# Seven half-size products for 9 of 11 pairs of feature blocks in a half-step FFN

## The chip, the core and the metric

The kernel runs on one core of a Trainium2 chip. The metric is the device time of one execution in microseconds. The engines named here are PE (TensorE, the matmuls), PEld (its weight loads), DVE (VectorE), ACT (ScalarE), POOL (GpSimd) and SP (SyncE, which issues most transfers). SBUF is the on-chip memory, PSUM the memory into which PE sums.

## The reference

The kernel computes two layers of an encoder for 512 tokens of width 1024. Each layer has three sublayers: a half-step FFN, a mixer, a second half-step FFN. The change is in the FFNs, whose core is

```
h = modulate(x, shift, scale)                       # x * (1 + scale) + shift, (512, 1024)
gate, up = jnp.split(h @ w_in, 2, axis=-1)          # w_in (1024, 2 * 2816)
y = (jax.nn.silu(gate) * up) @ w_out                # w_out (2816, 1024)
x = layer_norm(ALPHA * x + 0.5 * g * y, ln_g, ln_b)
```

Shift, scale and g of every sublayer come from a vector c: `mod = silu(c) @ ada_w[l] + ada_b[l]`, with ada_w[l] of 1024 x 9216. The mixer projects h by another matrix, runs a state-space scan, an attention and a short convolution on parts of it, and projects back. Everything is float32.

## The kernel before

**Precision.** A float32 product is made of three matmuls in float32r. Each operand is split into a high part (ACT copies it, rounded) and a low part (DVE subtracts the high part), and `mm3` adds low x high, high x low and high x high in PSUM. The helper `split` makes the parts of 1024 weights per partition, in tiles hi and li (input weights) or ho and lo (output weights).

**A half-step FFN** (`ffn`) goes over 11 pairs of blocks of 256 features: a pair is 256 gate columns and 256 up columns of w_in. For each, `cols_unit` loads two units of 1 MB (rows 0 to 1023, 256 columns), splits them in halves, and 2 x 2 blocks of 128 features by 512 tokens are summed in four PSUM banks over 8 row blocks: 96 matmuls of 512 columns. The first pair of a half-step runs on 256 tokens at a time, so that it can begin before the last token tile is ready. ACT makes silu of the gate (sg), DVE multiplies by up (af), and the result is split into ah and al. The pairs go in two groups (0 to 5, 6 to 10). After each group `out_proj` multiplies its features by the rows of w_out, for four token tiles and two halves of 512 columns, and `fold` adds gate times the result to x, two DVE instructions for each tile and half. After the second group come LayerNorm's statistics and normalization (`ln_norm`) and, by `modulate`, the transposed and modulated input hh, hl of the next sublayer.

**The affine of LayerNorm** (`x_affine`: x times g plus b) runs on POOL, 16 instructions of 128 x 512 to a sublayer, at pair 1 of an FFN and in the middle of a mixer.

**adaLN in the background.** `ada_acc` loads 1024 columns of ada_w in eight row blocks of 512 KB (ra) and sums them, weighted by silu(c), in two DVE instructions a block (acc). `ada_gate` and `ada_ss` (scale and shift) then split the sums and add them over the partitions on PE. These are Python generators; `begin` queues them at the start of an FFN, and `tick`, called at each of 33 weight units, advances them by a credit of 2.7 or 1.3 steps. A first FFN of a layer has three modules for itself and those after it, six sums of eight blocks in half-step 0; the last FFN has one sum.

**Buffers.** `rawp` holds two raw weight units of 8 KB per partition, `adap` two ada blocks, `whp` and `wlp` six high and six low halves each, `lp` 28 tiles of 2 KB for activations and vectors, `tp` nine temporaries. PSUM is two pools of four banks.

**Order.** Instructions are written in program order; a scheduler orders each engine by this priority among what its own timing finds ready, and adds the semaphores. Each engine then runs its list in order. Only the start of the first sublayer (`start`) is ordered by hand.

Of the kernel before, what the change touches and what calls it, by code (L numbers as in the profile page):

```python
# [8 lines left out]
F32 = mybir.dt.float32  # L9
# [18 lines left out]
NLONG = 28  # L28
NTMP = 9
NW = 6  # L30
# [3 lines left out]
CR = (2.7, 1.3)  # L34
WSZ = 1072
# [6 lines left out]
class InOrder:  # L42
    """An engine whose instructions are issued in program order while it is on."""
# [25 lines left out]
def trunk(ctx, tc, x, c, ln_in_g, ln_in_b, ada_w, ada_b, ffn1_w_in, ffn1_w_out,  # L69
# [8 lines left out]
    rawp = ctx.enter_context(tc.tile_pool(name="rawp", bufs=2))  # L78
    adap = ctx.enter_context(tc.tile_pool(name="adap", bufs=2))
# [6 lines left out]
    psa = ctx.enter_context(tc.tile_pool(name="psa", bufs=4, space=bass.MemoryType.PSUM))  # L86
    psb = ctx.enter_context(tc.tile_pool(name="psb", bufs=4, space=bass.MemoryType.PSUM))

    def pa(shape, name):
        return psa.tile(shape, F32, tag="a", name=name)  # L90

    def pb(shape, name):
        return psb.tile(shape, F32, tag="b", name=name)
# [128 lines left out]
    def ada_acc(l, col):  # L222
        """acc[p, f] = sum_k silu(c)[8p + k] * ada_w[l, 8p + k, col + f], row by row."""
        w = ada_w[l].rearrange("(p k) f -> p k f", k=KD)
        acc = [slot([P, 512], F32, f"acc{l}_{col}_{h}") for h in range(2)]
        for k in range(KD):
            raw = adap.tile([P, D], F32, tag="ra", name=f"ra{l}_{col}_{k}")
            sp.dma_start(raw, w[:, k, col:col + D])
            for h in range(2):
                rk = raw[:, h * 512:(h + 1) * 512]  # L230
                if k == 0:
                    after(dve.tensor_scalar(acc[h], rk, cT[:, 0:1], None, op0=ALU.mult), ln_done[0])
                else:
                    dve.scalar_tensor_tensor(acc[h], rk, cT[:, k:k + 1], acc[h],
                                             op0=ALU.mult, op1=ALU.add)
# [4 lines left out]
    def acc_split(acc):  # L240
        """The high and low part of each half."""
        parts = []
        los = adap.tile([P, 2, 512], F32R, tag="ra", name="gl")
        for h in range(2):
            hi, lo = tmp([P, 512], "gh", F32R), los[:, h]
            act.activation(hi, acc[h], AF.Copy)
            dve.tensor_tensor(lo, acc[h], hi.bitcast(F32), ALU.subtract)
# [3 lines left out]
    def acc_sum(ps, hi, lo):  # L251
        """The sum over the partitions, on every partition."""
# [7 lines left out]
    def mod_finish(s, a, b, psc, pss):  # L260
        """Features a*128 to b*128: scale and shift folded with the LayerNorm in front."""
# [39 lines left out]
    def ada_first(part, which):  # L301
        """The row blocks of the first sublayer's scale (1) or shift (0) for one range of features."""
        w = ada_w[0].rearrange("(p k) f -> p k f", k=KD)
        kk, nk = FIRST[part]
        n, nb = nk * P, (2, 1, 4)[part]
        c0 = which * D + kk * P
        raws = []
        for k in range(0, KD, nb):
            if part > 0:
                raw = slot([P, nb, n], F32, f"rf{part}_{which}_{k}")  # L310
            else:
# [5 lines left out]
    def sum_first(part, raws):  # L317
        """The sums over the row blocks, one vector instruction at a time."""
# [49 lines left out]
    credit = [0.0, 0.0]  # L368

    def begin(*gens):  # L370
        """Queue background work, to be spread over the 33 weight units of a half-step FFN."""
        pending.extend(gens)
        credit[0] = 0.0
        credit[1] = len(pending) and CR[0] if len(gens) > 2 else CR[1]

    def tick():
        credit[0] += credit[1]
        while pending and credit[0] >= 1:
            try:
# [4 lines left out]
                pending.pop(0)  # L384

# [8 lines left out]
    def load(w, c0, r0, k, n, name):  # L394
        """Rows r0 to r0 + 128 k, columns c0 to c0 + n, as [128, k, n]."""
        raw = rawp.tile([P, 2048], F32, tag="raw", name="r" + name)
        v = raw[:, :k * n].rearrange("p (k f) -> p k f", f=n)
        sp.dma_start(v, w[r0:r0 + k * P, c0:c0 + n].rearrange("(k p) f -> p k f", p=P))
        return v

    last = [None]

    def split(v, name, prev=None):
        """One half unit, any view [128, a, b] of raw weights, as high and low parts."""
        a, b = v.shape[1], v.shape[2]
        wh = whp.tile([P, WSZ], F32R, tag="wh", name="h" + name)[:, :a * b].rearrange("p (a b) -> p a b", b=b)
        wl = wlp.tile([P, WSZ], F32R, tag="wl", name="l" + name)[:, :a * b].rearrange("p (a b) -> p a b", b=b)
# [4 lines left out]
    def cols_unit(w, c0, name, prev=None):  # L412
        """256 columns of a [1024, .] matrix, two halves [128, 8, 128]."""
        v = load(w, c0, 0, KD, 256, name)
        return [split(v[:, :, j * P:(j + 1) * P], f"{name}_{j}", prev) for j in range(2)]

    def rows_unit(w, r0, c0, nk, name, prev=None):
        """128 nk rows by 512 columns, halves [128, 2, 512]."""
        v = load(w, c0, r0, nk, 512, name)
        return [split(v[:, 2 * j:2 * j + 2, :], f"{name}_{j}", prev) for j in range(nk // 2)]  # L420
# [8 lines left out]
    def ln_stat(t, h, st, piece=None):  # L429
        """Statistics of 512 columns, or of one half of them."""  # L430
# [17 lines left out]
    def finish(t, st):  # L448
        """The last LayerNorm, stored."""
# [9 lines left out]
    def ln_norm(t, st):  # L459
        """xt[t] <- (xt[t] - mean) * rstd."""  # L460
# [5 lines left out]
    def modulate(s, t, qq=(0, 1), prev=None):  # L466
        """hT[:, :, t] = the transposed modulation of xt[t] for sublayer s."""
        ts = slice(t * P, (t + 1) * P)
        for q in qq:
# [7 lines left out]
            hf = tmp([P, 4, P], f"hf{s}_{t}_{q}")  # L477
# [13 lines left out]
    def modulate_first(kk, ps):  # L491
        """hT[:, kk, :] for the first sublayer; yields before the vector part."""
        hf = tmp([P, T], f"hf0_{kk}")
# [3 lines left out]
        ln_done[0] = dve.tensor_tensor(hT[1][:, kk, :], hf, hT[0][:, kk, :].bitcast(F32), ALU.subtract)  # L497

# [4 lines left out]
    def ln_in(t):  # L503
        """The first LayerNorm of one token tile; yields between its vector parts."""
# [10 lines left out]
    def start():  # L515
        """Up to the first pair of the first sublayer, by ranges of features."""
# [10 lines left out]
        v = [load(ffn1_w_in[0], 0, 0, KD, 256, "i0_0_0")]  # L527
        raws.append(ada_first(1, 1))
        v.append(load(ffn1_w_in[0], DFF, 0, KD, 256, "i0_0_1"))
        raws[1] += ada_first(1, 0)  # L530
        raws.append(ada_first(2, 1) + ada_first(2, 0))
        v.append(load(ffn1_w_in[0], 256, 0, KD, 256, "i0_1_0"))
# [9 lines left out]
        def lo(which, j):  # L542
            units[which].append(split(v[which][:, :, j * P:(j + 1) * P], f"{("i0_0_0", "i0_0_1", "i0_1_0")[which]}_{j}"))
# [9 lines left out]
        def products(k, whiches=(0, 1)):  # L553
            for which in whiches:
                for j in range(2):
                    wh, wl = units[which][j]
                    mm3(banks[which][j], wh[:, k, :], wl[:, k, :],
                        hT[0][:, k, :], hT[1][:, k, :], k == 0, k == KD - 1)
# [26 lines left out]
        lo(0, 1)  # L585
# [10 lines left out]
        lo(1, 0)  # L596
# [22 lines left out]
        lo(2, 1)  # L619
# [4 lines left out]
        return banks, units[2]  # L624

    def x_affine(s, eng):
# [558 lines left out]
```

## Time and profile before

| | |
|---|---|
| device time, median of 2 runs | 2028.8 us (2028.63 to 2028.97) |
| span of the profiled execution | 2026.3 us |
| around the span, against the median | 2.5 us |
| matmuls | 9462 |
| DVE, ACT, POOL busy | 1190, 689, 218 us |
| moved by the transfers | 264 MB |

The profile names instructions by the tile that they write and read (`pf<-hh,hi` is a matmul into pf with the moving operand hh and the weights hi). Nearly all instructions are issued through one helper on line 52, so groups are told apart by tiles, not lines. A mean duration contains the time that an instruction spends in the pipeline beside its neighbours; the price of one instruction in a row of equal ones is the distance of their starts.

### The profile page before, as it was taken

What the parts mean: (1) busy time and instruction counts of PE and PEld (TensorE: products, weight loads), DVE (VectorE), ACT (ScalarE), POOL (GpSimd) and SP (SyncE); (2) the same over time, 40 slices, a digit from 0 to 9 for tenths busy, and PEclk for the clock granted to TensorE, in tenths of its full rate; (3) what the DMA queues carried; (4) which work ended last, traced back from release to release, by engine and by line L of the source; (5) the groups of instructions that cost most, each with busy time, mean ns of one, the idle gap of its engine ahead of it and who ended that gap; (6) DMA issues with size and microseconds to landing.
All of it is one profiled execution on the core that took longest, in us unless ns stands there. A gap on an engine that the chain in (4) does not pass through costs nothing.

```text
span 2026.3 us, 23498 instructions
## 1 busy us (share of the span) xinstructions
PE 1980.4 (98%) x9462; PEld 1624.8 (80%) x9462; DVE 1190.0 (59%) x1728; ACT 688.5 (34%) x1092; POOL 218.2 (11%) x182
## 2 busy tenths in 40 slices
PE   5999999999999999999999999999999999999998
PEld 4777878898877888888898788888977798888887
DVE  8896663467666655543477757436666575433336
ACT  3332132164454422122152322323544453222220
POOL 0230000007000040000004000000350004000000
PEclk9999999999999999999999999999999999999999
DMA  9765552333211544432345746322322144223331
GB/s 322 232 208 208 177 166 73 95 92 117 83 63 53 182 155 158 149 106 92 104 162 173 240 157 235 104 84 81 122 80 73 53 137 136 102 84 103 104 104 42
DMA packets 178540, 263.98 MB, mean 130 GB/s; under 512 B 9612, under 2 KB 124672, under 8 KB 178432
## 3 DMA queue, kind: packets, MB, share of 16 engines
q1 hardware_dynamic: 173936, 254.97, 37.7%
q10 hardware_dynamic: 4496, 7.52, 1.2%
q8 instruction: 74, 1.21, 0.2%
q14 instruction: 34, 0.28, 0.0%
HBM read 260.37 MB, written 2.10 MB: 130 GB/s over the span
## 4 chain that ended last, share of the span: by engine, by line
PE 85%; DVE 7%; DMA 4%; ACT 2%; issue 1%; POOL 0%; POOLq 0%; SPq 0%; DVEq 0%; ACTq 0%
PE pf L52 42%; PE po L52 26%; DMA ra<-in_ada_w_dram 4%; DVE acc L52 2%; PE pz L52 2%; PE pv L52 1%; PE pfo L52 1%; PE ptr L52 1%; DVE li L52 1%; PE pjm1x L52 1%; PE pS L52 1%; DVE af L52 1%; PE py L52 1%; PE pjm1sx L52 1%; PE pjm4sx L52 1%
## 5 line engine op out<-in xcount | busy, mean ns | idle before, releaser
L52 PE MATMUL pf<-hh,li 128*128 128x512 f32 (+1 forms) x1504 | 574.5, 382 | 1.3 <-DVE li L52 1.0
L52 PE MATMUL pf<-hl,hi 128*128 128x512 f32 (+1 forms) x1504 | 571.2, 380 | 0.2 <-DVE hl L52 0.2
L52 PE MATMUL pf<-hh,hi 128*128 128x512 f32 (+1 forms) x1504 | 570.7, 379 | 0.0
L52 DVE TENSOR_TENSOR li<-ri,hi 128x1024 fp32r<-128x1024 f32 x176 | 224.0, 1278 | 187.4 <-ACT hi L52 187.2
L52 PEld LDWEIGHTS pf<-hh,li 128*128 128x128 f32 x1504 | 283.3, 188 | 58.5 <-DVE li L52 1.7
L52 PEld LDWEIGHTS pf<-hl,hi 128*128 128x128 f32 x1504 | 284.8, 189 | 56.1 <-DVE hl L52 0.8
L52 PEld LDWEIGHTS pf<-hh,hi 128*128 128x128 f32 x1504 | 283.5, 188 | 57.7
L52 ACT ACTIVATE hi<-ri 128x1024 fp32r<-128x1024 f32 x176 | 185.4, 1059 | 317.4 <-PE pf L52 203.7
L52 PE MATMUL po<-ho,al 128*128 128x512 f32 (+1 forms) x704 | 276.6, 393 | 0.0
L52 PE MATMUL po<-ho,ah 128*128 128x512 f32 (+1 forms) x704 | 275.3, 391 | 0.0
L52 PE MATMUL po<-lo,ah 128*128 128x512 f32 (+1 forms) x704 | 274.7, 390 | 0.0
L52 DVE TENSOR_TENSOR lo<-ro,ho 128x1024 fp32r<-128x1024 f32 x104 | 127.2, 1223 | 215.3 <-ACT ho L52 215.2
L52 ACT ACTIVATE ho<-ro 128x1024 fp32r<-128x1024 f32 x104 | 110.1, 1058 | 293.1 <-PE po L52 166.6
L52 DVE SCALAR_TENSOR_TENSOR acc<-ra,cT,acc 128x512 f32<-128x512 f32 x224 | 171.6, 810 | 62.2 <-DMA ra<-in_ada_w_dram 61.9
L445 POOL TENSOR_TENSOR rs<-ve,mhalf 128x1 f32<-128x1 f32 x28 | 17.3, 619 | 1296.8 <-DVE ve L52 1277.8
L52 PEld LDWEIGHTS po<-ho,ah 128*128 128x128 f32 x704 | 132.1, 188 | 30.6
L52 PEld LDWEIGHTS po<-lo,ah 128*128 128x128 f32 x704 | 132.3, 188 | 29.6
L52 PEld LDWEIGHTS po<-ho,al 128*128 128x128 f32 x704 | 132.2, 188 | 29.6 <-DVE dg L52 0.3
L52 ACT ACTIVATE sg<-pf 128x512 f32<-128x512 f32 x88 | 52.4, 595 | 293.9 <-PE pf L52 276.8
L52 DVE TENSOR_TENSOR af<-sg,pf 128x512 f32<-128x512 f32 x88 | 60.2, 685 | 150.2 <-PE pf L52 147.3
L52 ACT ACTIVATE hf<-ptr,modB,modA 128x128 f32<-128x128 f32 (+1 forms) x168 | 66.8, 486 | 97.2 <-PE ptr L52 81.7
L632 POOL TENSOR_TENSOR x<-x,lng 128x512 f32<-128x512 f32 x48 | 76.3, 1613 | 215.3 <-DMA lng<-in_ln_g_dram 211.1
(391 smaller groups left out, 2448.0 us busy)
## 6 DMA issues: line engine op xcount, KB each, us to landing
ri<-in_ffn_w_in_dram SPq DMA_DIRECT2D x88, 1024.0 KB, 5.0
ra<-in_ada_w_dram SPq DMA_DIRECT2D x128, 512.0 KB, 4.5
ro<-in_ffn_w_out_dram SPq DMA_DIRECT2D x40, 1024.0 KB, 5.0
ro<-in_mix_w_out_dram SPq DMA_DIRECT2D x8, 1024.0 KB, 4.9
rf<-in_ada_w_dram SPq DMA_DIRECT2D x8, 512.0 KB, 8.6
ro<-in_ffn_w_out_dram SPq DMA_DIRECT2D x8, 512.0 KB, 3.6
rf<-in_ada_w_dram SPq DMA_DIRECT2D x16, 192.0 KB, 7.0
gate<-in_ada_b_dram SPq DMA_DIRECT2D x12, 256.0 KB, 5.8
```

The costliest lines, as they stand in the source:

```text
L52: ins = f(*a, **k)
L445: pool.tensor_tensor(rs, ve, mhalf[:, 0:1], ALU.pow)
L632: eng.tensor_tensor(xh, xh, aff[s, "g", h], ALU.mult)
```

## The change

**Seven products.** For pairs 2 to 10 of each half-step the product of a pair is treated as a 2 x 2 block product: the weights are gate and up by the lower and upper 512 rows, the activations the lower and upper 512 features by left and right 256 tokens. It is made of seven half-size products (512 rows, 256 features, 256 tokens) in place of eight, in Winograd's form. Four of the activation operands (t1 to t4) are differences, made once per half-step by `input_sums`, after pair 1, and split. Of the weights' sums, two (s3, s1) are made by a plain load and a second, accumulating transfer from POOL's queue; two more are made by DVE. PSUM tiles px, py and pw hold the sums; px goes on accumulating after ACT has copied what stands in it. The halves of the result are negative, and so `whole` (pairs 0 and 1, computed as before) negates too, and `fold` multiplies by -0.5.

**Order.** A pair is a generator of seven steps; the last three steps of a pair alternate with the first four of the next in its group, and the last pair of a group ends alone. There are four groups (0 to 2, 3 to 5, 6 and 7, 8 to 10), so `out_proj` and `fold` run four times per half-step. A tick comes after each step; the credit is 1.0 or 0.7.

**Buffers.** Raw weights, ada blocks, the unsplit input of an FFN and some mixer tiles share nine tiles of 4 KB (512 KB over all partitions), weights are loaded in units of 512 KB, split parts have five buffers each, `lp` has 15, and a new pool of six 4 KB tiles holds the operands t1 to t3 and mixer tiles. PSUM's pools are closed and opened anew for each sublayer: eight banks in one pool for an FFN, twice four for a mixer.

**Moved.** The affine runs on DVE, in four parts. The gate of each layer's first FFN but the first is summed one half-step earlier. In `out_proj` of the last group the halves of a token tile follow each other.

```diff
-NLONG = 28
+NLONG = 15
-NW = 6
+NW = 5
+NRAW = 9
+GROUPS = (range(0, 3), range(3, 6), range(6, 8), range(8, NPAIR))
-CR = (2.7, 1.3)
+CR = (1.0, 0.7)
...
+    def input_sums(s):
...
+        for n in ("t3", "t1", "t2", "t4"):
+            for a in range(2):
+                f = made[n, a] = tmp(shape, f"f{n}{s}_{a}")
+                if n == "t3":
+                    dve.tensor_tensor(f, block(1, 1, a), block(0, 1, a), ALU.subtract)
+                elif n == "t1":
+                    dve.tensor_tensor(f, block(0, 0, a), block(0, 1, a), ALU.subtract)
+                else:
+                    of, b = (("t1", block(1, 1, a)), ("t2", block(1, 0, a)))[n == "t4"]
+                    dve.scalar_tensor_tensor(f, made[of, a], -1.0, b, op0=ALU.mult, op1=ALU.subtract)
+                hi, lo = (piece(v, a) for v in ops[n])
+                act.activation(hi, f, AF.Copy)
+                dve.tensor_tensor(lo, f, hi.bitcast(F32), ALU.subtract)
...
-                eng.tensor_tensor(xh, xh, aff[s, "g", h], ALU.mult)
-                eng.tensor_tensor(xh, xh, aff[s, "b", h], ALU.add)
+                dve.tensor_tensor(xh, xh, aff[s, "g", h], ALU.mult)
+                dve.tensor_tensor(xh, xh, aff[s, "b", h], ALU.add)
+            yield
...
+        def seven(jp):
+            c0, name = jp * 256, f"i{s}_{jp}"
+            a11 = load(w_in, c0, 0, 4, 256, name + "a")
+            a12 = load(w_in, c0, 512, 4, 256, name + "b")
+            s3 = load(w_in, DFF + c0, 0, 4, 256, name + "c")
+            pool.dma_start(s3, rows_of(w_in, c0, 0, 4, 256), accum_op=ALU.add)
+            s1 = load(w_in, DFF + c0, 0, 4, 256, name + "d")
+            pool.dma_start(s1, rows_of(w_in, DFF + c0, 512, 4, 256), accum_op=ALU.add)
+            a22 = load(w_in, DFF + c0, 512, 4, 256, name + "e")
...
+            px, py, pw = (pp([P, 2, H2], f"p{n}{s}_{jp}") for n, pp in (("x", pa), ("y", pb), ("w", pa)))
...
+            def prepare():
+                i = len(ready)
+                if i == 3:
+                    sums.append(raw4([P, 4, 256], "s" + name))
+                    dve.tensor_tensor(sums[0], s1, a11, ALU.add)
+                elif i == 5:
+                    dve.tensor_tensor(sums[0], sums[0], a12, ALU.add)
+                if i < 7:
+                    v = (a11, a12, s3, sums and sums[0], s1, sums and sums[0], a22)[i]
+                    ready.append(split(v, name + "abcfdge"[i]))
+
+            prepare()
+            prepare()
+            product(px, ready[0], "11", True)
+            u1 = tmp([P, 2, H2], "u1")
+            act.activation(u1, px, AF.Copy)
+            yield
+            prepare()
+            product(py, ready[1], "21", True)
+            dve.tensor_tensor(u1, u1, py, ALU.add)
+            act.activation(u1, u1, AF.Silu)
+            yield
+            prepare()
+            product(pw, ready[2], "t3", True)
+            yield
+            prepare()
+            product(px, ready[3], "t2", False)
+            u2 = tmp([P, 2, H2], "u2")
+            act.activation(u2, px, AF.Copy)
+            yield
+            prepare()
+            product(px, ready[4], "t1", False)
+            u4 = tmp([P, 2, H2], "u4")
+            act.activation(u4, px, AF.Copy)
+            dve.tensor_tensor(u4, u4, pw, ALU.add)
+            yield
+            prepare()
+            product(px, ready[5], "22", False)
+            sg = tmp([P, 2, H2], "sg")
+            act.activation(sg, px, AF.Silu)
+            dve.tensor_tensor(u4, u4, sg, ALU.mult)
+            store(1, u4)
+            yield
+            product(pw, ready[6], "t4", False)
+            dve.tensor_tensor(u2, u2, pw, ALU.add)
+            dve.tensor_tensor(u2, u2, u1, ALU.mult)
+            store(0, u2)
...
+                cur = seven(jp)
+                for g in (cur, prev, cur, prev, cur, prev, cur) if prev else (cur,) * 4:
+                    next(g)
+                    tick()
...
+            for _ in range(3):
+                next(prev)
...
-            begin(ada_gate(s), ada_ss(s + 1), ada_gate(s + 1), ada_ss(s + 2))
+            begin(*([ada_gate(0)] if s == 0 else []), ada_ss(s + 1), ada_gate(s + 1), ada_ss(s + 2))
...
-            begin(ada_gate(s), *([ada_ss(s + 1)] if s < 5 else []))
+            begin(ada_gate(s), *([ada_ss(s + 1), ada_gate(s + 1)] if s < 5 else []))
```

`product` makes 24 matmuls of 256 columns (2 feature blocks, 4 row blocks, 3 parts). `store` splits one token half of the result into ah and al.

More of the change, by code (lines that the diff above doesn't have):

```diff
@@ L308, in ada_first @@
         for k in range(0, KD, nb):
-            if part > 0:
+            if part == 1 and which == 0:
                 raw = slot([P, nb, n], F32, f"rf{part}_{which}_{k}")
+            elif part > 0:
+                raw = big([P, nb, n], F32, f"rf{part}_{which}_{k}")
             else:
@@ new lines, in whole @@
+                    if (s, jp, which) == (0, 1, 0):
+                        units.append([next_unit[1], split(load(w_in, jp * 256, 512, 4, 256, "i0_1_0_1"), "i0_1_0_1")])
+                    else:
+                        units.append(cols_unit(w_in, which * DFF + jp * 256, f"i{s}_{jp}_{which}"))
+                    banks.append([pa([P, T], f"pf{s}_{jp}_{which}_{j}") for j in range(2)])
+                    tick()
+                n = H2 if jp == 0 else T
+                order = [(a, a + n, j, which) for a in range(0, T, n) for which in range(2) for j in range(2)]
@@ new lines, in whole, with product, store @@
+            return out
+        def seven(jp):
[7 more added lines that the diff above has]
+            a22 = load(w_in, DFF + c0, 512, 4, 256, name + "e")
+            def product(ps, w, n, first):
+                wh, wl = w
+                rh, rl = ops[n]
+                for j in range(2):
+                    js = slice(j * P, (j + 1) * P)
+                    for k in range(4):
+                        i = (j, k)
+                        for x, y, st in ((wl, rh, first and i == (0, 0)), (wh, rl, False)):
+                            pe.matmul(ps[:, j, :], x[:, k, js], y[:, k, :], start=st, stop=False,
+                                      skip_group_check=True)
+                        pe.matmul(ps[:, j, :], wh[:, k, js], rh[:, k, :], start=False, stop=i == (1, 3),
+                                  skip_group_check=True)
+            px, py, pw = (pp([P, 2, H2], f"p{n}{s}_{jp}") for n, pp in (("x", pa), ("y", pb), ("w", pa)))
+            halves = [None, None]
+            def store(th, f):
+                ah = slot([P, 2, H2], F32R, f"ah{s}_{jp}_{th}")
+                al = slot([P, 2, H2], F32R, f"al{s}_{jp}_{th}")
+                act.activation(ah, f, AF.Copy)
+                dve.tensor_tensor(al, f, ah.bitcast(F32), ALU.subtract)
+                halves[th] = ah, al
+            ready, sums = [], []
+            def prepare():
[44 more added lines that the diff above has]
+            store(0, u2)
+            for j in range(2):
+                acts.append(lambda t, j=j: tuple(v[:, j, (t % 2) * P:(t % 2 + 1) * P] for v in halves[t // 2]))
+            yield
@@ L690, in ffn @@
+        for gi, grp in enumerate(GROUPS):
+            acts = []
+            prev = None
+            for jp in grp:
+                if jp < 2:
+                    acts += whole(jp)
+                    if jp == 1:
+                        ops.update(input_sums(s))
+                    next(affine)
+                    next(affine)
+                    if s == 0 and jp == 0:
                         masks()
@@ L697, in ffn, with out_proj @@
                     neg_a()
-            last = gi == 1
-            if last:
-                if s == 5:
-                    ln_vectors(6)
-            out_proj(s, w_out, grp[0] * 256, acts, True, not last, last)
-    def out_proj(s, w_out, r0, acts, half, first, last):
+                prev = cur
+            for _ in range(3):
+                next(prev)
+            last = grp is GROUPS[-1]
+            if last and s == 5:
+                ln_vectors(6)
+            out_proj(s, w_out, grp[0] * 256, acts, True, gi == 0, last, 2)
+    def out_proj(s, w_out, r0, acts, half, first, last, head):
+        while s not in gates:
+            tick()
         n = len(acts)
@@ L772, in conv_silu @@
         def conv_silu(ci, dst):
+            pair = big([P, 2, T], F32, f"cv{s}_{ci}")
             def epi(j, ps):
@@ L870, in mixer @@
         feat(C_C, f"m{s}c", conv_silu(6, xbc), halves=True)
-        x_affine(s, pool)
+        affine = x_affine(s)
+        next(affine)
+        next(affine)
         feat(C_XS, f"m{s}x0", conv_silu(0, xbc))
+        next(affine)
+        next(affine)
         feat(C_XS + 256, f"m{s}x1", conv_silu(2, xbc))
```

301 lines of the change are left out of this document (177 added, 124 removed).

## The prediction

> **What bounds the kernel now.** I read the page first: busy time per engine, the slices, the chain.
>
> ```profile
> span 2026.3 us, 23498 instructions
> PE 1980.4 (98%) x9462; PEld 1624.8 (80%) x9462; DVE 1190.0 (59%) x1728; ACT 688.5 (34%) x1092; POOL 218.2 (11%) x182
> ...
> GB/s 322 232 208 208 177 166 73 95 92 117 83 63 53 182 155 158 149 106 92 104 162 173 240 157 235 104 84 81 122 80 73 53 137 136 102 84 103 104 104 42
> ...
> PE 85%; DVE 7%; DMA 4%; ACT 2%; issue 1%; POOL 0%; POOLq 0%; SPq 0%; DVEq 0%; ACTq 0%
> ```
>
> PE is busy for 98% of the span and is 85% of the chain, so the number of columns streamed sets the time and a cut in columns is worth its full price until another engine runs out. The transfers peak at 322 GB/s, in the first slice only. The next view is the windows of the six stages: half-step 0, mixer, half-steps 2 and 3, mixer, half-step 5 (columns: window, its length, then busy PE, PEld, DVE, ACT, POOL with counts, clock, DMA share, GB/s).
>
> ```profile
> 0.00:420.00 420.00, 391.16 (x1695) 315.48 (x1696) 277.26 (x409) 130.49 (x172) 34.20 (x39) 1.00 0.54 179
> 420.00:657.00 237.00, 234.25 (x1291) 192.34 (x1290) 158.45 (x285) 116.54 (x237) 49.50 (x41) 1.00 0.27 87
> 657.00:1030.00 373.00, 373.00 (x1730) 308.08 (x1729) 191.67 (x241) 111.97 (x157) 27.56 (x20) 1.00 0.38 129
> 1030.00:1412.00 382.00, 378.68 (x1735) 310.64 (x1734) 234.80 (x308) 115.15 (x162) 27.63 (x20) 1.00 0.48 158
> 1649.00:2026.00 377.00, 369.12 (x1730) 305.81 (x1728) 168.96 (x206) 97.82 (x129) 29.78 (x21) 1.00 0.31 104
> ```
>
> PE has no idle time to give back outside the start (420 - 391 = 29 us). DVE, the next engine, differs: 277 us of 420 in half-step 0, where six of the sixteen adaLN sums run, 169 of 377 in half-step 5, where one does.
>
> **The gain on PE.** The chain gives the time per product at both widths (start, length, count).
>
> ```profile
> 1649.87 5.59 PE pf L52 x48
> ...
> 1656.33 83.38 PE pf L52 x432
> 1740.63 44.35 PE pf L52 x192
> ```
>
> The 192 are 512 columns wide: 44.35 / 192 = 0.231 us. The 48 are 256 wide: 0.1165 us. The 432 are the other 144 narrow ones and 288 wide ones: 144 x 0.1165 + 288 x 0.231 = 83.3, as the row has, so narrow products hold half the time of wide ones in a long run too. A pair of blocks is now 2 (gate, up) x 2 x 8 x 3 = 96 wide products, 22.2 us. By seven half-size products it is 7 x 2 x 4 x 3 = 168 narrow ones, 19.6 us. That is 2.6 us less for each of 9 x 4 = 36 pairs: **-94 us**. The output products stay 528 per half-step.
>
> **What DVE gets.** Its price per instruction is the distance of starts where it runs back to back (start, length).
>
> ```profile
> 246.43 1.28 DVE L52 SCALAR_TENSOR_TENSOR gy<-po,gate 128x512 f32<-128x512 f32 x2
> 247.63 1.28 DVE L52 SCALAR_TENSOR_TENSOR x<-x,gy 128x512 f32<-128x512 f32 x2
> ...
> 254.41 1.40 DVE L52 SCALAR_TENSOR_TENSOR acc<-ra,cT,acc 128x512 f32<-128x512 f32 x2
> 255.73 2.35 DVE L52 TENSOR_TENSOR li<-ri,hi 128x1024 fp32r<-128x1024 f32 x2
> 258.00 1.40 DVE L52 SCALAR_TENSOR_TENSOR acc<-ra,cT,acc 128x512 f32<-128x512 f32 x2
> ...
> 104.13 6.89 DVE L52 SCALAR_TENSOR_TENSOR acc<-ra,cT,acc 128x512 f32<-128x512 f32 x4
> 110.94 1.77 DVE L52 TENSOR_TENSOR al<-af,ah 128x512 fp32r<-128x512 f32 x1
> ```
>
> Two instructions of 512 in 1.20 us: 0.60 each. A sum step 0.66 (254.41 to 255.73, two). A pass of 1024 1.135 (255.73 to 258.00, two). A pair had 4 splits and 4 instructions of 512: 6.9 us. It gets 7 splits, 2 sums of 1024 and 7 instructions of 512: 14.4 us, +7.5. Per half-step: pairs 9 x 7.5 = 67; the four input sums 16 x 0.60 = 10; 16 more folds of two instructions, since four groups fold instead of two, 19; the affine of LayerNorm, which moves from POOL, 16 x 0.60 = 10. Against that, what POOL cost DVE goes: the last two rows lie beside POOL's affine, where four sum steps take 6.8 us instead of 2.65.
>
> ```profile
> L52 DVE TENSOR_TENSOR li<-ri,hi 128x1024 fp32r<-128x1024 f32 x176 | 224.0, 1278 | 187.4 <-ACT hi L52 187.2
> L52 DVE SCALAR_TENSOR_TENSOR acc<-ra,cT,acc 128x512 f32<-128x512 f32 x224 | 171.6, 810 | 62.2 <-DMA ra<-in_ada_w_dram 61.9
> L633 POOL TENSOR_TENSOR x<-x,lnb 128x512 f32<-128x512 f32 x48 | 78.6, 1661 | 0.2
> ```
>
> The means are 1278 and 810 ns; undisturbed ones would be about 1210 and 740, so some 28 us over the kernel, 6 per half-step. Net +100 us of DVE per half-step; gate 3's sum (14 us) also moves from half-step 3 to 2. Half-step 0: 377 us of DVE in 420 - 23.5 = 396; half-step 2: 306 in 350; half-step 3: 321 in 358; half-step 5: 269 in 354. DVE stays below PE in each, but in half-step 0 by 5% only.
>
> [...]
>
> [...]
>
> **Where DVE and the transfers are short: under the adaLN sums.** The background work is spread by one sum step (two instructions, one 512 KB load) to a tick, and a tick now comes with each half-size product. A product is 24 x 0.1165 = 2.80 us of PE. In it DVE has 14.4 / 7 = 2.06, plus 2 x 0.66 = 1.32: 3.38 us. Its transfers are a weight quarter and an ada block, 1.05 MB, which at the 322 GB/s of the first slice takes 3.26 us. Both are over 2.80, so in these stretches a product costs 0.58 us too much. By the ticks in the code (4, 18, 11, 18 in the four groups, about 4 in an output product) such stretches are some 42 products in half-step 0, 22 in half-step 2, 35 in half-step 3, none in 5: 99 x 0.58 = 57 us; the high and low parts and the row sums that end each ada block (about 3 us, 11 blocks) bring 90. The output products give some of it back: PE needs 144 x 0.231 = 33 us for a group of three pairs, in which DVE has 6 splits and 16 folding instructions, 16 us. But only five split buffers let it run ahead, 5.7 us, in about nine groups: -50. I take **+40**, between 0 (all of it put off) and 90.
>
> **New waits.** px is summed into three times more after its first copy: a product must wait until ACT has copied what the one before left. Between two pairs the products alternate, and 2.8 us of the other pair hide it. In the last pair of a group they follow each other twice.
>
> ```profile
> L52 ACT ACTIVATE hi<-ri 128x1024 fp32r<-128x1024 f32 x176 | 185.4, 1059 | 317.4 <-PE pf L52 203.7 <-PE po L52 104.8 <-DMA ri<-in_ffn_w_in_dram 8.9
> ...
> L52 ACT ACTIVATE sg<-pf 128x512 f32<-128x512 f32 x88 | 52.4, 595 | 293.9 <-PE pf L52 276.8 <-DMA ra<-in_ada_w_dram 13.2 <-DMA lnb<-in_ln_b_dram 3.9
> ```
>
> A copy of 512 from PSUM is like sg, 0.6 us; with the drain of the product and two signals I estimate 1.0 us, and 1.6 when a split (1.06) stands in front on ACT. 4 groups x 4 half-steps x 2 = 32 waits; nothing but the output products can fill them. **+16**, between 0 and 51. The PSUM pools are closed and opened at each of five borders of sublayers: if the next one waits for the last fold (1.2 us and signals), 1.6 us each, **+8**, between 0 and 15. ACT itself has 7 x 1.06 + 7 x 0.6 = 11.6 us to a pair of 19.6. The two mixers change their buffers, and the affine's 10 us of DVE lie where DVE is busy for 158 us of 237: 0, between -6 and +20. The start of half-step 0 loads the same bytes, split by rows instead of columns: 0.
>
> **The sums by transfer.** An accumulating transfer follows its plain one, on POOL's queue, and no row of this trace shows one. What it holds up on POOL while it waits for the plain load is only LayerNorm's power at a half-step's end, ahead of two whole pairs that have no such transfer.
>
> ```profile
> ri<-in_ffn_w_in_dram SPq DMA_DIRECT2D x88, 1024.0 KB, 5.0
> ra<-in_ada_w_dram SPq DMA_DIRECT2D x128, 512.0 KB, 4.5
> ...
> rf<-in_ada_w_dram SPq DMA_DIRECT2D x8, 512.0 KB, 8.6
> ```
>
> For the same 512 KB the rows are 4.5 and, with the queues full, 8.6 us; I bound it by 4.5 and 17 (twice 8.6, as it reads its target too) and take 8. If its load starts with that of the pair's first quarter, 7.2 us (5.0 and a split of 2.2) ahead of the first product, the third product stands four products later, at 18.4 us; less 5.0 and 2.2 that leaves 11.2 us. At 8 nothing waits. In the lone pair of a group only two products precede: 12.8 - 7.2 = 5.6 us, so about 2.4 us late, 4 times a half-step at most, half of it covered by loads that run ahead in the output products: **+8** of the 16 lone starts, between 0 and 40.
>
> **Sum.** -94 + 40 + 16 + 8 + 8 = -22 on the span of 2026.3: 2004. The runs have a median of 2028.8, 2.5 above the span: **2007 us**.
>
> **Rivals.** (a) PE stays the bound: the scheduler lets the adaLN steps fall behind where DVE is short, since nothing needs most of them before the half-step's end. For it: by the stage sums DVE fits everywhere. Against it: in half-step 0 it fits by 5%, and DVE already sat idle 62 us until ada blocks came, in order, with splits behind them. The terms then are 10 for the sums, 8 + 8 for waits and borders: 2028.8 - 94 + 26 = 1961. (b) Slower: the nine raw buffers of 512 KB hold a pair's five quarters and its sum together with ada blocks and, until pair 1, four input tiles; the plain load starts late, the accumulation ends later, and PE waits at the third product of every pair. It decides where the accumulation takes over 11.2 us: each us beyond is 36 us, and from 13 us on (2007 + 1.8 x 36) the change is slower by over 2%; at 14.5, 2007 + 119 = 2126. Against it: half-step 5 moves 104 GB/s now. [...] (c) The gain isn't there: weight loads (1625 us of 1980) bound the narrow products in long runs. The 144 in a row speak against it; at 0.125 us instead of 0.1165, 36 x 168 x 0.0085 = 51 us go, 2058.
>
> **Chances.** Forecast (1988 to 2045) 0.45; (a) 0.38; (b) 0.13; (c) 0.04. 2% is 41 us, about what a measurement of this kernel can tell from no change; (a) lies below 1988, (b) above 2069. With the forecast's edges: faster 0.40, same 0.46, slower 0.14. The range reaches down to 1945, where (a) has only 10 of its 26 us, and up to 2060, past the forecast's upper costs and (c), leaving out most of (b). The forecast's own range is 1985 to 2045.
>
> **What would show it.** PE's busy time should be near 1890 and its products 36 x 72 = 2592 more. Half-step 5 should shrink by nearly all its 23 us, half-step 0 by least, with DVE over 90% busy and PE waiting for splits there. The adaLN blocks should end PE's waits through DVE. If all four half-steps shrink alike by 20 us or more, (a) is right; if PE waits for the third product's weights in half-step 5 too, (b). A landing time of the accumulating transfer above 11 us, or a new wait at each step in the middle of a group, would make the prediction wrong.

## The result and the profile after

The changed kernel takes 2154.05 us (2150.74 to 2157.35) against 2028.8: the ratio is 1.0617, with a 95% interval of 1.0579 to 1.0656. It is slower by 6%, and lies outside the predicted range. Its page:

```profile
span 2155.4 us, 30326 instructions
PE 1955.6 (91%) x12042; PEld 1746.5 (81%) x12042; DVE 1582.4 (73%) x2306; ACT 879.3 (41%) x1342; POOL 157.4 (7%) x158
...
q1 hardware_dynamic: 195440, 273.86, 39.8%
q0 software_dynamic: 38016, 37.75, 11.5%
...
PE 68%; DVE 16%; DMA 8%; issue 4%; ACT 3%; SPq 1%; POOL 0%; ACTq 0%; POOLq 0%; DVEq 0%
```

PE is still the busiest engine, but it is no longer the bound: 2155.4 - 1955.6 = 200 us pass without a running matmul (46 before), and the chain of waits now runs through DVE and transfers for 24% (11% before). PE's busy time went down by 25 us only. The six stages (columns as before, the clock is the third number from the end):

```profile
0.00:465.00 465.00, 384.13 (x2348) 345.13 (x2348) 367.43 (x547) 179.56 (x244) 29.27 (x41) 0.95 0.68 198
465.00:709.00 244.00, 234.83 (x1290) 194.06 (x1290) 165.11 (x304) 114.84 (x237) 25.63 (x26) 0.99 0.22 68
709.00:1113.00 404.00, 368.91 (x2376) 338.67 (x2376) 301.92 (x396) 162.12 (x223) 25.72 (x22) 0.96 0.61 167
1113.00:1524.00 411.00, 371.17 (x2380) 340.00 (x2380) 315.13 (x423) 162.52 (x224) 24.79 (x21) 0.95 0.64 179
1773.00:2155.00 382.00, 356.23 (x2358) 329.51 (x2358) 267.18 (x337) 145.24 (x184) 26.78 (x22) 0.96 0.54 142
```

Half-steps 0, 2, 3 and 5 grew by 45, 31, 29 and 5 us: most where six adaLN sums run, least where one does, and about alike with four and five. The two mixers grew as well, by 7 and 12 us. The clock, 1.00 in each half-step before, is 0.95 to 0.96. The granted clock was half in 25 stretches, 170 us in all, each behind an idle time of PE; matmuls ran for 109 us of that, so it cost about 54 us. What PE waited for (us in total, times, longest):

```profile
PE px L53 <- DVE li_2a L53: 50.3, 4, 19.5
PE px L53 <- ACT u L53: 19.1, 19, 3.5
PE pf L53 <- DVE li L53: 16.1, 3, 5.4
...
PE px L53 <- DVE li_5f L53: 8.6, 3, 3.0
PE pw L53 <- DVE li_5c L53: 8.3, 3, 3.9
PE po L53 <- DVE al L53: 7.8, 4, 6.4
PE pv L53 <- ACT hf L53: 7.2, 2, 3.6
```

The largest is one place in each half-step: the first seven-product pair (2) waits for its first split, li_2a. The chain in half-step 5 shows why (start, length):

```profile
1802.72 7.16 DMA lnb<-in_ln_b_dram
...
1827.51 3.01 DVE x L53 x5
1830.53 1.15 DVE li_2a L53
1831.67 0.14 issue
1831.81 5.43 PE px L53 x24
...
1838.17 2.86 PE py L53 x24
```

The load of a LayerNorm vector (lnb) takes 7.16 us of the chain, and DVE stands idle for 3.2 us at this vector and its neighbour lng; then affine, input sums and the tail of pair 1 run on DVE back to back, and li_2a stands behind them all. PE has been idle for 9.7 us when it starts, and its first 24 products take 5.43 us at half clock, where the next 24 take 2.86.

The second pattern is DVE held by an accumulating transfer, here in half-step 5 between pairs 7 and 8:

```profile
2007.19 1.24 DVE li_7g L53
2008.42 0.02 issue
2008.44 4.75 DMA ri_8d<-in_ffn_w_in_dram
...
2013.72 0.81 DMA ri_8d<-in_ffn_w_in_dram
2014.54 7.51 issue
2022.05 0.09 DVE si L53
...
2023.19 1.22 DVE lo L53
2024.41 0.61 DVE u L53
2025.02 0.04 issue
2025.06 4.52 PE pw L53 x24
```

At the head of DVE's queue stands si, the sum that pair 8 needs for its fourth product, waiting for s1 (ri_8d), whose accumulating transfer is issued at 2013.7. Its plain load had been issued only at 2008.4: the chain goes back to li_7g, where DVE reads pair 7's sum for the last time, which stands in a raw buffer too. So a late DVE also delays the load for which it then waits. Behind si stand lo and u, for which the trace shows no wait of their own, and PE's next product into pw waits for u; it then runs at half clock. DVE stands idle ahead of si like this nine times, for 3.0 to 7.9 us each and 49 in all (the trace names the transfer for three of them and nothing for six). That transfer's time from issue to landing, and the two ends of the medians by tile (last column, us):

```profile
DMA to landing us min/median/max: 8.2/8.2/8.2
```
```profile
ri_2c<-in_ffn_w_in_dram POOLq DMA_DIRECT2D x4, 512.0 KB, 6.4
...
ri_5d<-in_ffn_w_in_dram POOLq DMA_DIRECT2D x4, 512.0 KB, 12.3
```

The plain 512 KB loads of w_in take 5.5 us in the row for the first two pairs, and 3.5 to 8.3 in those of the others that have a median. By the rows of the two queues, accumulating costs 11.5 / 37.75 = 0.30% of the engines' span per MB, plain loading 39.8 / 273.86 = 0.145%: twice as much.

### The profile page after: what moved, and what is told of

It reads as the page before. It is cut to its first block, busy times and chain, and to the rows that moved or that the text cites. A ratio compares the mean times of both kernels' runs of the same rounds, so it can differ in the third digit from the quotient of the medians.

```text
span 2155.4 us, 30326 instructions
## 1 busy us (share of the span) xinstructions
PE 1955.6 (91%) x12042; PEld 1746.5 (81%) x12042; DVE 1582.4 (73%) x2306; ACT 879.3 (41%) x1342; POOL 157.4 (7%) x158
## 3 DMA queue, kind: packets, MB, share of 16 engines
q1 hardware_dynamic: 195440, 273.86, 39.8%
q0 software_dynamic: 38016, 37.75, 11.5%
## 4 chain that ended last, share of the span: by engine, by line
PE 68%; DVE 16%; DMA 8%; issue 4%; ACT 3%; SPq 1%; POOL 0%; ACTq 0%; POOLq 0%; DVEq 0%
PE po L53 24%; PE px L53 13%; PE pw L53 7%; PE py L53 4%; PE pf L53 3%; DVE acc L53 3%; DVE x L53 2%; PE pz L53 2%; PE pv L53 1%; DVE u L53 1%; DMA ri_4c<-in_ffn_w_in_dram 1%; DMA lnb<-in_ln_b_dram 1%; PE pjm1x L53 1%; PE pjm4x L53 1%; PE pfo L53 1%
## 5 line engine op out<-in xcount | busy, mean ns | idle before, releaser
L53 PE MATMUL po<-ho,al 128*128 128x512 f32 x698 | 274.5, 394 | 8.6 <-DVE al L53 7.8
L53 PE MATMUL po<-lo,ah 128*128 128x512 f32 x698 | 273.4, 392 | 4.7 <-DVE lo L53 4.7
L53 PE MATMUL po<-ho,ah 128*128 128x512 f32 x698 | 272.4, 392 | 0.0
L53 PEld LDWEIGHTS po<-ho,al 128*128 128x128 f32 x698 | 132.0, 189 | 38.7 <-DVE al L53 11.5
L53 PE MATMUL pf<-hh,li 128*128 128x256 f32 (+1 forms) x352 | 120.9, 343 | 16.7 <-DVE li L53 16.1
L53 PE MATMUL pf<-hl,hi 128*128 128x256 f32 (+1 forms) x352 | 119.7, 340 | 0.8 <-DVE hl L53 0.8
L53 PE MATMUL pf<-hh,hi 128*128 128x256 f32 (+1 forms) x352 | 119.2, 339 | 0.0
L53 DVE SCALAR_TENSOR_TENSOR gy<-po,gate 128x512 f32<-128x512 f32 x127 | 84.0, 685 | 43.9 <-PE po L53 43.8
L53 PEld LDWEIGHTS pf<-hh,li 128*128 128x128 f32 x352 | 69.9, 199 | 23.7 <-issue 16.7
L53 PEld LDWEIGHTS pf<-hl,hi 128*128 128x128 f32 x352 | 69.8, 198 | 7.8 <-DVE hl L53 1.9
L53 PEld LDWEIGHTS pf<-hh,hi 128*128 128x128 f32 x352 | 69.6, 198 | 6.1
```

What stands on the lines that cost most here:

```text
L53: ins = f(*a, **k)
```

## The experiments

My theory: each pair's DVE work and transfers come late where adaLN sums, accumulating transfers and the affine stand in the same queues, and PE pays for that at half clock. The rivals: the frame (buffers, groups, and the borders, where one sublayer ends and the next begins) costs it, or the half-size products themselves do. The time of the kernel before on the chip in question ran from 2023 to 2033 us, so each run is given by its distance from it (the change: +125). Runs without an interval are single ones; under some 10 us only their traces are read.

**One cost at a time.** e1: seven of eight blocks of each adaLN sum left out, in the changed kernel; e2: the same in the kernel before.

```
         for k in range(KD):
+            if k > 0:
+                yield acc
+                continue
             raw = raw4([P, D], f"ra{l}_{col}_{k}")
```

> The changed kernel with one of the eight row blocks in each adaLN sum; the other seven blocks are left out, loads and sums, the ticks stay. Theory A (DVE and the transfers are short only under the adaLN sums): half-steps 0, 2 and 3 lose most of the waits that half-step 5 does not have, 2155 goes to about 2070, half-step 5 stays at 382 us. Theory B (the sums by accumulating transfer come late and hold DVE's queue) and theory C (a burst of affine and input sums on DVE makes pair 2 late at every half-step): both are in half-step 5 too, so little goes, about 2130.

> The kernel before with one of the eight row blocks in each adaLN sum, the other seven left out. PE is the bound there, so every theory expects the time of before, 2020 to 2029 us; a gain would mean that adaLN cost something before the change already, and the gain of e1 is to be read less that.

e1 took 2073.58 us, 50 over the kernel before: 75 us of the change's 125 went. e2 took 2016.01 us, 8 us under it, which a single run hardly tells from nothing. So the sums were nearly free before and cost some 75 us beside the seven products. By the traces half-steps 0, 2, 3 and 5 shrink by 38, 22, 22 and 5 us in e1: the cost lies where the sums run.

e3 leaves out the accumulating half of s3 and s1 (their sums lack a term); e4 makes both sums by two more passes of DVE from four plain loads.

```
             s3 = load(w_in, DFF + c0, 0, 4, 256, name + "c")
-            pool.dma_start(s3, rows_of(w_in, c0, 0, 4, 256), accum_op=ALU.add)
```

> The changed kernel without the 72 accumulating transfers: s3 and s1 hold the plain load only, everything else runs. Theory B: the waits at the sums go in all four half-steps, about 60 to 80 us, 2155 to about 2085, and half-step 5 from 382 to about 360. Theory A: only the transfers are relieved, 20 to 30 us, in half-steps 0, 2 and 3. Theory C: under 10 us.

> The changed kernel with s3 and s1 made by DVE from the four quarters that are loaded anyway: 4 loads per pair in place of 5 plain and 2 accumulating, 2 passes of 1024 more on DVE (2.3 us a pair, 82 us in all). Theory B: faster than the changed kernel, about 2110, and half-step 5 near 365. Theory A: slower where DVE was short, so half-steps 0, 2 and 3 by 10 us each or more, about 2180 in all.

e3: 2106.0 us, +82, so the transfers cost 43, in all four half-steps (16, 9, 18 and 8 us by the traces). e4: 2144.31 us, +121. It loads four quarters for a pair, one less than e3's kernel, yet only 4 us are won, since DVE is busy for 1662.9 us then, 80 more: the sums are paid on either engine.

e5 leaves out the affine; e8 loads its vectors ahead of the first pair and leaves the affine itself where it was written, behind pairs 0 and 1.

```
-                dve.tensor_tensor(xh, xh, aff[s, "g", h], ALU.mult)
-                dve.tensor_tensor(xh, xh, aff[s, "b", h], ALU.add)
```

> The changed kernel without the affine of LayerNorm (the 96 DVE instructions are left out; its vectors are still loaded). Theory C (at pair 1 the affine waits on DVE for its vectors, and with the input sums behind it makes a burst that holds up pair 2's first split): the wait of px for the first split of pair 2, 50 us in four half-steps, falls to under 20, and the slow clock behind it with it: about 45 us less. Theory A (DVE short under the adaLN sums): 58 us less of DVE, of which the half-steps 0, 2 and 3 give back 20, half-step 5 nothing.

> The changed kernel with the LayerNorm vectors loaded ahead of an FFN's first pair and the affine after it, in three parts behind pair 0 and 1. Theory C, if the waiting transfer is the cause: the wait for pair 2's first split falls by 6 us in each half-step, with the slow clock about 30 us in all. If the burst of DVE work itself is the cause, under 10 us. Theories A, B and D: nothing.

```profile
PE px L53 <- DVE li_2a L53: 16.0, 1, 16.0
```

That row is e5's (2130.54 us, +101): the wait at pair 2 is gone but for half-step 0, and 24 us with it. In e8 (2142.58 us, +113) it is 13.2 us, once too; half-step 5 takes 366 us, but half-step 0 lengthens by 13, 6 of them at its start (the first product into pf comes at 35.7 us, not 29.7).

**Moving the background.** e7 spreads the adaLN sums over mixers as well (4, 3, 3, 3, 3, 0 by stage), with ticks in the mixers and a credit of 1.0 throughout; e6 has six split buffers, seven temporaries and eight raw buffers.

```
-            begin(ada_gate(s), *([ada_ss(s + 1), ada_gate(s + 1)] if s < 5 else []))
+            if s < 5:
+                begin(ada_ss(s + 1), ada_gate(s + 1))
...
+            begin(ada_ss(s + 1), ada_gate(s + 1))
             mixer(s, l)
```

> The changed kernel with the adaLN sums spread over the mixers too: 4, 3, 3, 3, 3, 0 sums in the six sublayers in place of 6, 0, 4, 5, 0, 1. Theory A: the FFNs have 10 of 16 sums left, so about three eighths of the 80 us that e1 gave come back, and half-step 5 is unchanged: about 2120, if the mixers, where DVE is busy 166 of 245 us, take 42 us of DVE each for nothing. If they don't, they grow by 10 us or more each and the total stays at about 2145.

> The changed kernel with six split buffers in place of five, paid for by seven temporaries in place of nine and eight raw buffers in place of nine. Theory D (at the borders all five split buffers are held by the last output product until its last matmul, so the next sublayer's first split starts only then): the gaps of 5.4 us ahead of pf and 3.6 us ahead of pv, 23 us in five borders, and the slow clock behind them go, about 30 us less. If the fewer raw buffers count (theory B, transfers late), half-steps get longer elsewhere by as much.

e7: 2199.14 us, +169. The half-steps win 6 to 17 us each and each mixer loses about 40 (285 us): there is no free room in the mixers either. e6: 2191.53 us, +162. The waits at the borders are the same (16.1 and 7.2 us), while px waits 34.4 us for ACT's copies instead of 19.1: a sixth split buffer doesn't help, and the two temporaries and the raw buffer that pay for it are missed (which of them, this run can't say). That theory fell.

**The frame without the seven products.** e9 makes all pairs whole.

```
-                if jp < 2:
+                if jp < 11:
                     acts += whole(jp)
```

> All eleven pairs of blocks by eight products, as the first two are, in everything else of the changed kernel: buffers pooled by size (17 long and 8 raw ones instead of 15 and 9, which the other order needs), four groups, the affine of LayerNorm on VectorE, PSUM pools per sublayer; a pair gives 6 ticks instead of 7. It takes the seven products and their sums away and leaves the frame. If the loss comes from what the seven products ask of VectorE and of the transfers, this stands near the kernel before: 2015 to 2045 us. If the frame (four groups, buffers, affine, borders) carries a large part of it, 2060 us or more, with idle time of TensorE in half-step 0 and behind LayerNorm as in the changed kernel.

```profile
span 2039.0 us, 24071 instructions
PE 1967.4 (96%) x9450; PEld 1641.2 (80%) x9450; DVE 1277.9 (63%) x1954; ACT 696.8 (34%) x1094; POOL 64.0 (3%) x86
```

2040.76 us, +8. The seven products with their sums cost the other 117. The frame's +8 is a balance: the wide matmuls have become faster in it, and without that it costs 45 (e16, below). Its mixers take 247 and 248 us, against 237 before, so the mixers' growth belongs to the frame. By its trace 9 stretches at half clock cost 21 us and 72 us are idle.

**The three costs together.** e10 has one adaLN block, no accumulating transfers, no affine; e11 keeps the affine. Their edits are those of e1, e3 and e5.

> The changed kernel with one of eight blocks of each adaLN sum, without the accumulating transfers, and without the affine of LayerNorm: the three costs that single runs showed as 80, 48 and 24 us, left out together. If they are separate costs, 2154 - 152 = 2002 us; if all of them take from the same room of VectorE, less goes: 2030 us. If the half-size products as such carry a cost (their order, the waits of px, the borders), it doesn't come below 2016 us, which the kernel before took with one block. If the products give what their rate says (76 us), it goes to 2016 - 76 = 1940 us at best, plus some 35 us of waits at borders and lone pairs: 1975 us.

> The same, but with the affine of LayerNorm: only the adaLN blocks and the accumulating transfers are left out. Separate costs: 2154 - 128 = 2026 us. If both stand for one cause, sums that come late on VectorE's queue while the transfers are full, taking the second away gains less than its 48 us: 2040 to 2060 us. The difference to the run without affine should be 10 to 24 us and lie behind LayerNorm.

```profile
span 2010.1 us, 29501 instructions
PE 1924.9 (96%) x12042; PEld 1722.5 (86%) x12042; DVE 1384.7 (69%) x1986; ACT 877.5 (44%) x1342; POOL 64.4 (3%) x86
```

e10: 2011.8 us, 21 under the kernel before; e11: 2035.05 us, +2. Together they take away 147 us; apart 75 + 43 + 24 = 142. So they are separate costs to a good part. But with all three gone the kernel stands only 13 us below e2's (-21 against -8), which has one adaLN block as well. By the traces PE is still idle for 85 us (39 in e2) and loses 28 to half clock; the gain on PE itself may be smaller than predicted too.

e12 uses the seven products in half-step 5 alone, with e8's order.

```
-                if jp < 2:
+                if jp < {0: 11, 2: 11, 3: 11, 5: 2}[s]:
```

> Seven products in half-step 5 alone (where one adaLN sum runs), eight in half-steps 0, 2 and 3; the LayerNorm vectors loaded ahead of the first pair and its affine behind that pair; 16 long and 8 temporary buffers. If room on VectorE decides, half-step 5 takes 360 to 368 us (377 before, 382 in the changed kernel) and the whole stands 10 to 15 us below the run with all blocks whole, at 2005 to 2030 us. If the half-size products cost as much as they give even there, half-step 5 stays at 377 us or above.

2046.76 us, +14. Half-step 5 takes 368 us, against 376.6 in e9: it is shorter by 9 us there, seven products and early vectors together. The whole stands 6 us above e9, not 10 to 15 below: half-step 0 is longer by 9.

**What a product costs.** The chains of e9 and of the change give the rates (start, length, count):

```profile
1711.58 21.76 PE pf L53 x96
...
1765.98 65.28 PE pf L53 x288
```
```profile
104.44 2.88 PE py L53 x24
107.32 2.88 PE pw L53 x24
```

A wide product takes 65.28 / 288 = 0.2267 us in the new frame, not 0.231 (from start to start; in the kernel before a single one into pf lasts 394 to 397 ns in the mean); a narrow one 0.120, not 0.1165. The diff changes the distance between split buffers from 1072 elements (WSZ) to 1024, an edit that the description of the change leaves out. e16 puts 1072 into e9's kernel; e17 puts 1024 into the kernel before, whose mixers then split the value block in four pieces.

```
-WSZ = 1072
+WSZ = 1024
...
-            us.append(split(v, f"m{s}v{u}"))
+            us += [split(v[:, 2 * i:2 * i + 2, :], f"m{s}v{u}_{i}") for i in range(2)]
```

> All pairs by eight products as in the run with all blocks whole, with the split buffers 1072 elements apart as in the kernel before, not 1024 (and 8 temporary buffers for 9). If the distance of the weights in memory sets the time of a wide product, it is 0.231 us again and the span is about 30 us longer: 2070 us. If it is something else (the PSUM banks from one pool, the row halves), it stays at 0.2267 us and 2041 us.

> The kernel before with its split buffers 1024 elements apart instead of 1072; in the mixers the value block is split in four pieces instead of two so that it fits. If the distance of the split buffers alone sets the time of a product, wide products take 0.2267 us instead of 0.231, TensorE's 1980 us shrink by some 30 us, and since TensorE bounds this kernel the whole goes to 1995 to 2005 us, ahead of both kernels. If the rate belongs to the other frame, 2026 us as before.

e16: 2070.8 us, +45, and 66.53 / 288 = 0.231 again:

```profile
1790.94 66.53 PE pf L53 x288
```

e17's chain in half-step 2:

```profile
657.97 82.58 PE pf L52 x432
741.45 43.52 PE pf L52 x192
```

43.52 / 192 = 0.2267, and the 144 narrow ones among the 432 take (82.58 - 288 x 0.2267) / 144 = 0.120. The one edit sets both. It can also move the tiles of the pools that are opened behind the split buffers, moving operands among them; whether the distance or such a place does it, no run tells. e17 takes 2006.85 us, ratio 0.9909 (0.9892 to 0.9926): the fastest of all these kernels, ahead of before and after, by an edit that the change carried along.

**The borders.** At three entries to a half-step PE waits 5.4 us, at both entries to a mixer 3.6. e9's chain at one:

```profile
1030.97 0.45 PE ptr L53 x4
1031.42 0.02 issue
1031.45 1.85 ACT hf L53 x5
...
1034.87 0.95 ACT hi L53
1035.82 0.02 issue
1035.85 1.24 DVE li L53
1037.08 0.14 issue
1037.22 2.90 PE pf L53 x12
```

ACT makes the input of the last-but-one tile (hf) and only then the first split (hi). e13 (in the changed kernel) and e14 (in e9's) finish the first column half for all tiles first, so that split buffers come free, and split the first block ahead of that tile. e15 is e14 with seven products in half-step 5 and its vectors early; e18 is e14 with PSUM kept open from half-step 2 to 3.

```
-            out_proj(s, w_out, grp[0] * 256, acts, True, gi == 0, last, 2)
+            out_proj(s, w_out, grp[0] * 256, acts, True, gi == 0, last, len(acts))
...
+            if t == NT - 1 and s in (1, 2, 4):
+                pre[s + 1, 0, 0] = cols_unit(w, 0, f"i{s + 1}_0_0")
...
-        if s > 0:
+        if s > 0 and s != 3:                      # e18 alone
             new_psum(s, *((8,), (4, 4), (8,))[j])
```

> The changed kernel; in the last output product of a half-step the first column half is finished for all token tiles before the second starts (as the mixers do it), so that its split buffers come free, and the first gate block of the next half-step is split ahead of the last tile's LayerNorm instead of behind it. If the gaps of TensorE at the borders (16.1 us for the split, 7.2 us for the last tile's input) come from split buffers held to the end and from the order on ScalarE, they go, and with them part of the stretches at half clock behind them: 23 to 40 us less, 2115 to 2132 us. If the reopened PSUM pools hold the border, the gaps stay and the time is 2150 to 2160 us.

> The same two edits in the kernel with all pairs by eight products (2040.8 us). If the wide products keep their 0.2267 us there (0.231 in the kernel before, 32 us over all) and the border gaps go, 2041 - 23 - about 10 of half clock: 2000 to 2018 us, below the kernel before by 1%. If the gaps move to another place, 2030 to 2041 us.

> The same, with seven products in half-step 5 alone and its LayerNorm vectors loaded ahead of the first pair. Nine pairs times 1.6 us (96 x 0.2267 against 168 x 0.120) are 14 us of TensorE; by the run with seven in half-step 5 some 6 of them go in new waits. If that holds: 8 us below the run with all pairs whole. If the seven products cost more than they give once the borders are clear: the same or above.

> The kernel with all blocks whole and cleared borders, with the PSUM pool kept open from half-step 2 to 3 (both have one pool of eight banks). At that border TensorE waited 3.80 us for ScalarE's reading of the transposed tile. If the closing and opening of the pool is what makes the first product wait for it, this gap goes to under 1 us, and those at the two borders behind mixers (3.1 us each) stay; 2037 to 2043 us. If the banks' order within one pool does it, the gap stays at 3.8 us.

```profile
PE pf L53 <- ACT hf L53: 10.0, 3, 3.8
PE ptr L53 <- DVE x L53: 7.5, 3, 3.1
```
```profile
PE pf L53 <- ACT hf L53: 6.1, 2, 3.1
```

The first two rows are e14's (2044.6 us, ratio 1.0098, 1.0080 to 1.0116). The wait for the split is gone, but the first product now waits 3.1 to 3.8 us for ACT's reading of a transposed tile, though it uses only the two tiles before; and PE now waits for LayerNorm (x) too. So e14 isn't faster than e9, and the forecast of 2000 to 2018 us fell. The last row is e18's (2034.84 us, +9): where the pool stays open the 3.8 us wait is gone, two of 3.1 us stay. So at that border the reopened pool holds the first product, behind a first hindrance, the order of the splits. In the changed kernel the same edits make it slower: e13 takes 2187.45 us, +161, and PE waits 27.4 us for LayerNorm's x, ahead of which folds and statistics run back to back on DVE (for 11 us at the border before half-step 3). e15 takes 2038.72 us (1.0071, 1.0050 to 1.0092), 6 below e14, where early vectors may have a share.

## Why the prediction was wrong

The span grew by 129 us, where -22 was forecast: +154 of idle time, +53 of half clock, and about -77 for products, worked out from the traces as running time less half clock. The sum had 72 us of waits and a gain of 94 on PE, so it failed twice: the waits were sized by stage totals and by who needs a result, and the gain by the rates of the old buffers. Rival (a), that PE stays the bound, had a chance of 0.38; 200 us of idle PE speak against it.

- **The gain on PE: mis-sized.** Of the 77, e9's kernel has 32 without any half-size product. The seven products earned about 46 of the 94 predicted. The step that failed is 22.2 - 19.6 = 2.6 us a pair: with the new distance it is 96 x 0.2267 - 168 x 0.120 = 1.6 us, 58 for 36 pairs; where the other 12 went, no run shows. I read the rates of the old buffers and passed over WSZ in the diff. Rival (c) had the direction (0.120 against its 0.125), but e17 ties that time to the distance of the buffers; whether the weight loads from them carry it, no run shows.
- **What DVE gets: right.** 377, 306, 321 and 269 us were forecast for the half-steps; 367, 302, 315 and 267 came. With the affine off POOL, DVE's two means of 1278 and 810 ns became 1221 and 749 (my estimate was 1210 and 740). The sum has nothing for POOL's issuing of the 72 accumulating transfers, and the trace shows no cost of it on DVE: 53 of DVE's splits of 1024 ran beside such an issue and took 1.22 us, as the others did.
- **The adaLN stretches: too small.** 40 (0 to 90) against 75 in e1. The sum had taken 50 off 90 for what the output products give back; no run shows how much they did.
- **The sums by transfer: the step that failed most beside the gain.** 8 (0 to 40) against 43 in e3. The landing time, 6.4 to 12.3 us by the rows, was near the 8 us that I took; but I followed only who needs the weights, four products later. On DVE's queue the sum stands ahead of work of the other pair, so it is needed much earlier, as between pairs 7 and 8 above. With that, half-step 5 didn't shrink by 23 us; it grew by 5. The +8 doesn't follow from its own terms either: 16 starts of 2.4 us, half covered, are 19.
- **The affine: wrong place.** I priced it as 10 us of DVE's time in each sublayer, which seemed to fit. In the half-steps it and the input sums stand in one block ahead of pair 2: 24 us by e5.
- **The mixers: 0 (-6 to +20) in the sum.** They grew by 7 and 12 us, 19 in all.
- **The half clock: not in the sum.** The trace of before had two such stretches (3.4 us from 1151.9, and 6.0 from 2022.3, behind PE's last matmul); idle PE cost its gap and then again up to 2.6 us for 24 products. The stretches of the change measure 3.4, 6.8, 10.2 us and more, nearly all whole multiples of 3.4. How much idle time is needed, the trace doesn't settle: 2.31 us (until 874.7) was enough, while 2.34 us (until 295.5) passed at full clock.
- **The waits for px: right in total** (16, measured 19.1 in 19 waits; the 0.4 us beyond the copy's 0.6 was my estimate), in part by luck: only 8 us of it lie in the last pairs of a group, where I had put them all; three waits of 2.3 to 3.5 us in the middle of groups make up most of the rest. **The borders: mechanism right in part, size wrong**: 1.6 us each against 3.6 to 5.4, with half clock behind; e18 shows the pool, and the trace shows the split order in front of it.
- **Rival (b)** gave the nearest time, 2126, and a transfer was indeed one cause, but not by its condition, so the number is luck: PE did not wait for the third product in every pair, and landing times mostly stayed under its 11.2 us. Its first link is in the trace: plain loads that start late for want of a raw buffer, as at 2008.4 above.

Left open: how the costs of e1 and e3 divide between DVE's queue and the full transfers. And no run had the seven products without the reopened pools, nor at the old distance, where by their rates they would earn 2.6 us a pair.

## What to carry to other kernels

Where an engine takes its instructions in order, as DVE did here, one that waits for a late transfer delays what stands behind it (7.5 us between pairs 7 and 8): ask of each new wait not who needs its result, but what stands behind it, above all with two pairs interleaved. The changed kernel's half-steps have DVE busy for 70 to 79%, and PE still waited for it, above all behind blocks of added work; price the largest block ahead of PE's next input, and add the half clock behind a gap: past the start, each of PE's 18 idle times of 3.2 us and more had it here. And read every constant of a diff: the one that looked like tidying (1072 to 1024) made the kernel before 19 us faster by itself (e17), while the half-size products of the change lost more than they earned.

## What the runs showed of the hardware

- Changing the distance between split buffers changed the time of a matmul in float32r: 0.231 us at 1072 elements and 0.2267 at 1024 for 512 columns, but 0.117 (0.117 to 0.119 in e16) and 0.120 for 256. e16 and e17 show it in both directions. Why the two widths react oppositely, no run shows.
- An accumulating 512 KB transfer took 6.4 to 12.3 us to land (medians by tile) and twice the DMA engines' time per MB of a plain one (0.30% against 0.145% of their span).
- PE lost 54 us to half clock in 25 stretches of 170 us in all, though its busy share was 91%.
- POOL's issuing of an accumulating transfer didn't lengthen DVE's splits that ran beside it (1.22 us with and without).
